# Retention output in an encoder step: the products with v first, then one product per pair of heads with a state on the diagonal of a 128x128 block

## The chip, the cores and the metric

The kernel runs on one core of a Trainium2 chip. A time is device microseconds of one execution. The kernel before was run three times: median 1369.04 us, lowest 1367.47, highest 1370.69. One further execution was recorded by the hardware profiler; its records span 1362.0 us, and all rows shown here come from it. In the rows PE is TensorE, PEld its weight loads, DVE is VectorE, ACT is ScalarE, POOL is GpSimd, SP is SyncE.

## The reference, cut to what matters

Two layers run over 512 prompt frames and 32 sample frames. Each layer has three branches: attention, retention and a gated recurrence. The change touches retention alone, for 8 heads of 64 columns:

```python
inner = jnp.einsum('bnihd,bnjhd->bnhij', q, k) * decay
y_in = jnp.einsum('bnhij,bnjhe->bnihe', inner, v)
...
y_x = jnp.einsum('bnihd,nbhde,hi->bnihe', q, s_prev, xi)
return (y_in + y_x).reshape(b, t, h, d).astype(dt), s_final.astype(s0.dtype)
```

`y_in` is what a block of frames gives its own frames, through v. `y_x` is what all blocks before it give, through the state (64x64 for each head). The sum of both goes on to a normalization per head.

## The kernel before, in words

All activations lie with features on partitions and the 544 frames (512 and 32) along the free dimension. The kernel's main work is a long row of products with 128x128 blocks of weights (`block`, L244). Each float32 weight is split into a high and a low part, the cast on ScalarE (L200) and the difference on VectorE (L201), eight blocks of weights ahead of their use (`LEAD = 8`). A block is three products (high by high, high by low, low by high) for each of two halves of 272 columns, so six matmuls.

Everything else is side work: generators that are resumed between blocks. Each yields the number of blocks to pass before its next step, taken from the table `PACE`. So the order on each engine is written by the program, once, and an engine works its own list in order. A step's place is counted in blocks of weights; nothing in it depends on how long anything takes.

`ret_job` is the side work of retention. It runs once for each layer.

- It makes copies of v and k with frames on partitions (`vt`, `kt`; `vts`, `kts` for the 32 sample frames), through transposes (L322).
- It makes the products of k and v for each block of 128 frames and each head (L574), and copies them to `kv`, half of the tile named `states`.
- It takes the mean over a head's columns off v (POOL, L589 and L591), adds up and decays `kv` (L598, L599), and writes the centred states into `stc`, the other half of `states` (VectorE, L611 and L612). In `stc` head 2p lies on partitions 0 to 63 and head 2p+1 on 64 to 127, each 64 columns wide.
- For each of the four pairs p of heads: eight products of q and k (L635), their mask on VectorE (L638), seven blocks of weights later the output. The output's PSUM tile `pv` is one bank of 128 partitions by 512 columns: head 2p in the upper 64 partitions, 2p+1 in the lower. Block c of 128 columns gets a product with v for each head (L649: 128 rows of weights by 64 columns, 128 columns moved) and, where c > 0, a product with the state for each head (L652: 64 rows by 64 columns, 128 moved). The two kinds alternate. Then ScalarE copies the bank out (L654).
- For the sample frames the same in eight pairs of a product with v (L661: 32 rows by 64 columns, 32 moved) and one with the state (L663: 64 by 64, 32 moved), and a copy (L664).

The operands here are plain float32. The trace holds two PE records for each such product, for instance 128 records of L649 for its 64 products. Below a pass is one such record.

Rotary positions for q are put on beside it (`rope_tile`): a swap by DMA, products on VectorE (L545) and POOL (L546), a sum on VectorE (L548), a scale on POOL (L551, L552). Large tiles come from the pool `slab`, which has 15 places that are given out again when their last reader is done.

Of the kernel before, what the change touches and what calls it, by code (L numbers as in the profile page):

```python
# [13 lines left out]
MUL, ADD, SUB = ALU.mult, ALU.add, ALU.subtract  # L14
# [3 lines left out]
NP, NS = 512, 32  # L18
# [7 lines left out]

# [1 line left out]
BRANCH = {"A": 0, "B": 1, "C": 2}  # L28
# [4 lines left out]
def layer_units():  # L33
    """Units of 128 output features, in groups whose 128x128 blocks are taken in turn. wg stands for the
    recurrence's gates, two to a block, which are used beside the units that follow."""
    u = [[("pl", f)] for f in range(8)]
    u += [[("xr", 0), ("xr", 1)], [("wg", 0)], [("xr", 2)], [("xr", 3)]]
    u += [[("va", t)] for t in range(4)]
    for t in range(4):
        u += [[("qa", t)], [("ka", t)]]  # L40
    u += [[(k, t)] for k in ("kb", "vb", "qb") for t in range(4)]
    for br in "CAB":
        u += [[("z" + br.lower(), t)] for t in range(4)]
        for f in range(8):
            u += [[("g" + br, f)], [("b" + br, f)]]
    u += [[(k, f)] for k in ("wo", "pg") for f in range(8)]
    return u


def blocks_of(kind):  # L50
# [8 lines left out]
LEAD = 8  # L59
# a layer's last units, from this one on, take one half of the columns after the other  # L60
HELD = (6, 2)
WARM = (16, 30, 5)
# blocks to pass between the steps of the side work
PACE = {
# [5 lines left out]
# copies out of PSUM: 1 where the vector engine makes them, 2 where the two engines take turns  # L70
VEC = {"va": 0, "tok": 0, "p0": 0, "p1": 0, "pt": 0, "kv": 0, "pv": 1, "yb": 0}

# [1 line left out]
C_ID, C_O64, C_O1K, C_MK = 0, 128, 256, 384  # L74
# [5 lines left out]

# [1 line left out]
P_CW, P_CB, P_BA, P_BX, P_LAM, P_GN, P_LG, P_LB = 0, 16, 20, 24, 28, 32, 36, 44  # L82
# [29 lines left out]
def bc(ap, dims):  # L112
    """A view of a tile's part: its partitions, then `dims` as [step, count] from its first element."""
    return bass.AP(ap.tensor, ap.offset, [ap.ap[0], *dims])
# [3 lines left out]
def encoder(ctx: ExitStack, tc, xT, pT, W, RB, KC, VC, PAR, CST, o_y, o_k, o_v, o_rp, o_rs, o_cv, o_lr):  # L118
# [17 lines left out]
    def sl(name, dt=F32, shape=(128, 4, N)):  # L136
        return slab.tile(list(shape), dt, tag="slab", name=name)
# [12 lines left out]
    sp = cp.tile([128, 2, L, 4], F32, name="sp")  # L150
# [5 lines left out]

    # ---- side work: generators that are resumed between the blocks of the main products. Each yields the
    # number of blocks to pass before its next step. ----
    jobs = []
    clock = [0]  # L160
# [19 lines left out]

# [1 line left out]
    raw, parts, held = {}, {}, {}  # L182
# [41 lines left out]

    # the next layer's first chunks are split before the normalization takes the engines
    def split_ahead(l):
# [30 lines left out]

    # products that nobody reads keep the tensor engine's clock up where it waits
    def busy(n):
# [3 lines left out]

# [1 line left out]
    st = {"xh": [sl("xh", F32R) for _ in range(2)], "xl": [sl("xl", F32R) for _ in range(2)]}  # L265
# [26 lines left out]

    # 4 softplus(-lambda) and -8 softplus(-lambda)
    def decay_rates():
# [16 lines left out]

# [1 line left out]
    def layer(l, env, nxt):  # L313
# [10 lines left out]

        # token-major copy of a feature-major operand
        def tok_steps(src, tok, toks, d):
# [3 lines left out]

        # -- attention --
        def bias_loads(p):
# [40 lines left out]
        def attn_step(p, qs):  # L373
# [3 lines left out]
            now = [], []  # L377
            # the two heads' products lie in different rows of the array
            for j in range(2):
# [95 lines left out]

        # -- recurrence --
        W547 = NP + 3 + NS
# [32 lines left out]
        def lru_job():  # L510
            R, I, A = env["lru"]
            # s = tanh(4 sp r), a = exp(-8 sp r); 1 - a = s (1 + a), 1 - a^2 = (1 - a)(1 + a)
            for t in range(4):
                S.activation(A[:, t], R[:, t], AF.Exp, scale=sp[:, 1, l, t:t + 1])
                S.activation(R[:, t], R[:, t], AF.Tanh, scale=sp[:, 0, l, t:t + 1])
                yield PACE["lru0"]
            y = I
            for t in range(4):
                r, a = R[:, t], A[:, t]
                V.scalar_tensor_tensor(r, a, 1.0, r, ADD, MUL)  # L520
                V.tensor_scalar(a, r, -1.0, 1.0, MUL, ADD)
                V.scalar_tensor_tensor(r, a, 1.0, r, ADD, MUL)
                yield PACE["lru1"]
            for t in range(4):
                S.activation(R[:, t], R[:, t], AF.Sqrt)
                yield PACE["lru2"]
            for t in range(4):
                G.tensor_tensor(R[:, t], R[:, t], I[:, t], MUL)
                yield PACE["lru3"]
                V.tensor_tensor_scan(y[:, t, :NP], A[:, t, :NP], R[:, t, :NP], 0.0, MUL, ADD)  # L530
                V.tensor_tensor_scan(y[:, t, NP:], A[:, t, NP:], R[:, t, NP:], pcol(P_SL, t), MUL, ADD)
            yield 2
            env["yc"] = y
            Q.dma_start(out=o_lr[l, :, :, 0:1], in_=y[:, :, NP - 1:NP])
            Q.dma_start(out=o_lr[l, :, :, 1:2], in_=y[:, :, N - 1:N])

        # -- retention: q and k carry gamma^(i + 1) and gamma^-(j + 1), i and j counted in their block --
        def rope_tile(key, t, x):
# [17 lines left out]
        def ret_job():  # L556
# [7 lines left out]
            yield from tok_steps(KB, kt, kts, PACE["tok"])  # L564
            # states before the centering of v over a head's columns
            stt_ = sl("states", shape=(128, 2, 16, 64))
            kv, stc = stt_[:, 0], stt_[:, 1]
            kvs = tmp("kvs", (128, 4, 64))
# [41 lines left out]
            yield 3  # L610
            V.tensor_tensor(stc[:, :12], kv[:, :12], bc(smu[:, :12], [[1, 12], [0, 64]]), SUB)  # L611
            V.tensor_tensor(stc[:, 12:], s0, bc(smu[:, 12:], [[1, 4], [0, 64]]), SUB)  # L612
            yield 6
# [3 lines left out]
            mask = cst[:, C_MK:C_MK + 128]  # L617
            # sample
            ins = tmp("ins", (NS, 2, 4, 32))
# [9 lines left out]
            for p in range(4):  # L629
# [12 lines left out]
                yield PACE["y2"]  # L642
                pv = psum("pv")
                for c in range(4):
                    cc = slice(c * 128, c * 128 + 128)
                    for j in range(2):
                        r = slice(64 * j, 64 * j + 64)
                        h = 2 * p + j
                        T.matmul(pv[r, cc], lhsT=vt[:, c, h * 64:h * 64 + 64], rhs=inn[j][:, cc],  # L649
                                 start=True, stop=c == 0)  # L650
                        if c:
                            T.matmul(pv[r, cc], lhsT=stc[r, (c - 1) * 4 + p], rhs=QB[r, p, cc],  # L652
                                     start=False, stop=True)
                copy("yb")(QB[:, p, :NP], pv)  # L654
                yield PACE["y3"]
            pv = psum("pv")
            for h in range(8):
                q, j = h // 2, h % 2
                r = slice(64 * j, 64 * j + 64)
                o = pv[r, q * 32:q * 32 + 32]  # L660
                T.matmul(o, lhsT=vts[:, h * 64:h * 64 + 64], rhs=ins[:, j, q], start=True, stop=False,  # L661
                         tile_position=(0, 64 * j))
                T.matmul(o, lhsT=stc[r, 12 + q], rhs=QB[r, q, NP:], start=False, stop=True)  # L663
            S.copy(QB[:, :, NP:], pv[:, :128].rearrange("p (a b) -> p a b", a=4))  # L664
# [28 lines left out]

        # -- normalization: c, the mean over a quarter of the features, is taken off first; the sums of what is
        # left and of its squares give the mean and the variance. hf: the half of the columns, None for all. --
        def span(hf):
# [83 lines left out]

        # -- what is done with a unit's products --
        KEY = {"ka": "KT", "va": "VA", "qb": "QB", "kb": "KB", "vb": "VB"}
# [104 lines left out]

        # the embedding through its gate; running sums for the normalization
        def gate(t, ps, hf):
# [35 lines left out]

        # units of which one half of the columns is taken after the other; together: block by block of all of
        # them, or one unit after another
        def by_halves(units, together):
# [161 lines left out]
```

## Time and profile before

| | before |
|---|---|
| median of 3 runs | 1369.04 us (1367.47 to 1370.69) |
| profiled execution, span | 1362.0 us |
| its time beside the span | not recorded; the median is 7.0 us above the span |
| PE busy | 1337.0 us, 98%, 10847 instructions |
| PEld busy | 1284.8 us, 94% |
| DVE, ACT, POOL busy | 57%, 44%, 15% |
| mean granted TensorE clock | 0.994 |
| retention's products of the output | L649 x128, L652 x96, L661 x32, L663 x32 records |

A row of the timeline gives a start, a duration from the first start to the last end, the engine, the line, the operation, the tile it writes and reads, the rows*columns of weights, the moved partitions x columns, and how many were merged. Matmuls overlap: one that takes 0.27 us from start to end may have the next one start 0.06 us after it, so durations do not add up. What a stretch costs is read from starts: from the start of the row ahead of it to the start of a row behind it. The rows around 295 to 345 us are the four pairs and the sample frames of the first layer; around 963 to 1015 us are those of the second. The granted clock is a share of full speed in each slice.

### The profile page before, as it was taken

The numbers are of one execution on the slowest core, as the hardware profiler recorded it, in microseconds if no ns is written. First come the engines' busy times: TensorE is split into PE (matmuls) and PEld (weight loads), VectorE is DVE, ScalarE is ACT, GpSimd is POOL, SyncE is SP. The second block draws the span as 40 slices with busy tenths as digits, with TensorE's granted clock in tenths as the row PEclk, the third lists the DMA queues.
The fourth block names the chain that finished last, engine by engine and source line by source line (L and its number), as shares of the span: only waits on it lengthen the run. The fifth ranks groups of instructions, "written<-read, shape, count | busy, mean of one in ns | idle before, by whom it ended". The sixth has DMA issues, their size and how long they took to land.

```text
span 1362.0 us, 26929 instructions
## 1 busy us (share of the span) xinstructions
PE 1337.0 (98%) x10847; PEld 1284.8 (94%) x10847; DVE 780.5 (57%) x1659; ACT 596.8 (44%) x1491; POOL 197.7 (15%) x190
## 2 busy tenths in 40 slices
PE   9999999999999999999999999999999999999985
PEld 9999899997999999999899998999889999999985
DVE  5576563661664453467875756558328544445576
ACT  7765544421642243344476654444126333333343
POOL 0210122200101101002311102132001010110034
PEclk9999999999999999999999999999999999999998
DMA  7233513221122222223112453232112222222201
GB/s 287 63 126 94 175 61 98 87 71 47 63 94 94 93 79 84 103 94 125 63 63 100 86 167 98 76 98 82 50 48 93 94 79 93 78 94 93 93 17 66
DMA packets 44284, 124.95 MB, mean 92 GB/s; under 512 B 9344, under 2 KB 13696, under 8 KB 43520
## 3 DMA queue, kind: packets, MB, share of 16 engines
q1 hardware_dynamic: 44160, 123.24, 27.1%
q8 instruction: 85, 1.39, 0.4%
q14 instruction: 39, 0.32, 0.1%
HBM read 111.52 MB, written 7.24 MB: 87 GB/s over the span
## 4 chain that ended last, share of the span: by engine, by line
PE 88%; DVE 6%; ACT 3%; issue 2%; POOL 0%; DVEq 0%; ACTq 0%; POOLq 0%
PE mm L244 76%; PE pv L413 1%; PE pv L649 1%; PE sc L386 1%; PE pv L652 1%; PE tp L402 1%; ACT wh L200 1%; DVE wl L201 1%; PE sc L635 1%; PE tp L322 1%; DVE held L201 1%; PE mm L262 1%; DVE r L714 1%; DVE r L767 1%; DVE lru_i L530 1%
## 5 line engine op out<-in xcount | busy, mean ns | idle before, releaser
L201 DVE TENSOR_TENSOR wl<-raw,wh 128x256 fp32r<-128x256 f32 x704 | 308.7, 473 | 319.5 <-ACT wh L200 318.7
L244 PE MATMUL mm<-xh,wh 128*128 128x272 f32 x2144 | 456.2, 294 | 0.5 <-ACT xrp L829 0.5
L244 PE MATMUL mm<-xl,wh 128*128 128x272 f32 x2144 | 444.3, 288 | 0.0
L244 PE MATMUL mm<-xh,wl 128*128 128x272 f32 x2144 | 442.4, 287 | 0.4 <-DVE wl L201 0.4
L244 PEld LDWEIGHTS mm<-xh,wh 128*128 128x128 f32 x2144 | 335.1, 188 | 14.6 <-issue 10.6
L244 PEld LDWEIGHTS mm<-xh,wl 128*128 128x128 f32 x2144 | 336.6, 188 | 0.6 <-DVE wl L201 0.6
L244 PEld LDWEIGHTS mm<-xl,wh 128*128 128x128 f32 x2144 | 335.7, 188 | 0.0
L200 ACT CAST wh<-raw 128x256 fp32r<-128x256 f32 x704 | 251.1, 403 | 55.8 <-PE mm L244 52.8
L852 ACT ACTIVATE sg<-mm 128x544 f32<-128x544 f32 x48 | 30.1, 626 | 145.0 <-PE mm L244 145.0
L864 POOL TENSOR_TENSOR m<-m,sg 128x544 f32<-128x544 f32 x30 | 42.5, 1417 | 313.4 <-DVE sg L862 313.4
L244 PE MATMUL mm<-xh,held 128*128 128x272 f32 x320 | 64.8, 296 | 7.1 <-ACT sg L895 5.1
L347 ACT ACTIVATE sx<-sx,sst 128x128 f32<-128x128 f32 (+4 forms) x68 | 37.9, 558 | 68.5 <-DVE sst L345 65.7
L244 PEld LDWEIGHTS mm<-xh,held 128*128 128x128 f32 x320 | 51.7, 192 | 9.3 <-ACT sg L895 5.5
L244 PE MATMUL mm<-ml,wh 128*128 128x272 f32 x256 | 53.0, 288 | 0.0
L244 PE MATMUL mm<-mh,wh 128*128 128x272 f32 x256 | 52.9, 288 | 0.0
L244 PE MATMUL mm<-mh,wl 128*128 128x272 f32 x256 | 52.8, 287 | 0.0
L862 DVE TENSOR_TENSOR sg<-mm,sg 128x544 f32<-128x544 f32 x32 | 23.2, 725 | 41.5 <-PE mm L244 41.5
L244 PE MATMUL mm<-xl,held 128*128 128x272 f32 x160 | 46.7, 292 | 0.0
L255 ACT CAST xh<-r 128x544 fp32r<-128x544 f32 (+1 forms) x32 | 17.0, 532 | 67.6 <-DVE r L879 63.8
L244 PEld LDWEIGHTS mm<-mh,wl 128*128 128x128 f32 x256 | 40.2, 188 | 0.0
L244 PEld LDWEIGHTS mm<-ml,wh 128*128 128x128 f32 x256 | 40.1, 188 | 0.0
L688 POOL TENSOR_TENSOR QB<-QB,sq 128x544 f32<-128x544 f32 x8 | 10.9, 1366 | 200.9 <-DVE sq L686 190.5
(256 smaller groups left out, 1923.4 us busy)
## 6 DMA issues: line engine op xcount, KB each, us to landing
raw<-in_W SPq DMA_DIRECT2D x189, 512.0 KB, 3.2
bias<-in_RB SPq DMA_DIRECT2D x16, 256.0 KB, 4.2
x<-in_xT SPq DMA_DIRECT2D x4, 544.0 KB, 8.6
o_v<-VA SPq DMA_DIRECT2D x2, 1088.0 KB, 4.5
o_k<-KT SPq DMA_DIRECT2D x2, 1088.0 KB, 5.2
swap<-KB SPq DMA_DIRECT2D x32, 68.0 KB, 2.7
swap<-QB SPq DMA_DIRECT2D x32, 68.0 KB, 2.0
o_y<-r SPq DMA_DIRECT2D x6, 272.0 KB, 2.2
```

Of the source, the lines that this page charges most:

```text
L200: S.copy(h, t)
L201: V.tensor_tensor(lo, t, h.bitcast(F32), SUB)
L244: T.matmul(ps[:, hf, :H2], lhsT=w[:, n % 2, :], rhs=x[:, hf * H2:(hf + 1) * H2], start=first and i == 0, stop=last and i == 2)
L255: S.copy(h, src)
L262: T.matmul(ps[:, 0, :H2], lhsT=zero[:, :128], rhs=zero, start=True, stop=True)
L322: T.transpose(tp[:rows, t * 128:(t + 1) * 128], src[:, t, c0:c0 + rows], ident)
L347: S.activation(x, x, AF.Exp, bias=s[:, 0:1], scale=-1.0, accum_out=s[:, 1:2])
L386: T.matmul(scs[j][:, o:o + n], lhsT=q_[r, p, i * 128:i * 128 + 128], rhs=k_[r, p, :n], start=k == 0, stop=k == 2)
L402: T.transpose(tp[:, c:c + 128], xs[j][:, c:c + 128], ident)
L852: S.activation(halves(sg), pv, AF.Sigmoid)
L862: V.tensor_tensor(halves(sg), pv, halves(sg), MUL)
L864: (V if kind == "bB" and t == 7 else G).tensor_tensor(m, m, sg, ADD)
```

## The change

The states lie in a tile of their own, `std`, 16 blocks of 128x128. A block is for one pair of heads: head 2p's state in its upper left 64x64 quarter, head 2p+1's in its lower right one, and zeros in the two others. The zeros come from a memset on POOL ahead of the products of k and v. VectorE writes the quarters in four instructions of 64 partitions in place of two of 128. `kv` becomes a tile of its own.

The output of a pair begins with all eight products with v. The three products with a state follow: one for both heads, 128 rows by 128 columns. The first product in each half of the bank clears it, all others add to it, and the last ends the group: one accumulation group for the bank. The sample frames go the same way: eight products with v, then four with a state. Comments were taken out, too, and lines moved by four.

```diff
-            stt_ = sl("states", shape=(128, 2, 16, 64))
-            kv, stc = stt_[:, 0], stt_[:, 1]
+            kv = sl("kv", shape=(128, 16, 64))
+            std = sl("states", shape=(128, 16, 128))
+            G.memset(std, 0.0)
...
-            V.tensor_tensor(stc[:, :12], kv[:, :12], bc(smu[:, :12], [[1, 12], [0, 64]]), SUB)
-            V.tensor_tensor(stc[:, 12:], s0, bc(smu[:, 12:], [[1, 4], [0, 64]]), SUB)
+            for j in range(2):
+                r = slice(64 * j, 64 * j + 64)
+                V.tensor_tensor(std[r, :12, 64 * j:64 * j + 64], kv[r, :12], bc(smu[r, :12], [[1, 12], [0, 64]]), SUB)
+                V.tensor_tensor(std[r, 12:, 64 * j:64 * j + 64], s0[r], bc(smu[r, 12:], [[1, 4], [0, 64]]), SUB)
...
                 for c in range(4):
                     cc = slice(c * 128, c * 128 + 128)
                     for j in range(2):
-                        r = slice(64 * j, 64 * j + 64)
                         h = 2 * p + j
-                        T.matmul(pv[r, cc], lhsT=vt[:, c, h * 64:h * 64 + 64], rhs=inn[j][:, cc],
-                                 start=True, stop=c == 0)
-                        if c:
-                            T.matmul(pv[r, cc], lhsT=stc[r, (c - 1) * 4 + p], rhs=QB[r, p, cc],
-                                     start=False, stop=True)
+                        T.matmul(pv[64 * j:64 * j + 64, cc], lhsT=vt[:, c, h * 64:h * 64 + 64], rhs=inn[j][:, cc],
+                                 start=c == 0, stop=False)
+                for c in range(1, 4):
+                    cc = slice(c * 128, c * 128 + 128)
+                    T.matmul(pv[:, cc], lhsT=std[:, (c - 1) * 4 + p], rhs=QB[:, p, cc], start=False, stop=c == 3)
...
-            for h in range(8):
-                q, j = h // 2, h % 2
-                r = slice(64 * j, 64 * j + 64)
-                o = pv[r, q * 32:q * 32 + 32]
-                T.matmul(o, lhsT=vts[:, h * 64:h * 64 + 64], rhs=ins[:, j, q], start=True, stop=False,
-                         tile_position=(0, 64 * j))
-                T.matmul(o, lhsT=stc[r, 12 + q], rhs=QB[r, q, NP:], start=False, stop=True)
+            for q in range(4):
+                for j in range(2):
+                    h = 2 * q + j
+                    T.matmul(pv[64 * j:64 * j + 64, q * 32:q * 32 + 32], lhsT=vts[:, h * 64:h * 64 + 64],
+                             rhs=ins[:, j, q], start=q == 0, stop=False, tile_position=(0, 64 * j))
+            for q in range(4):
+                T.matmul(pv[:, q * 32:q * 32 + 32], lhsT=std[:, 12 + q], rhs=QB[:, q, NP:], start=False, stop=q == 3)
```

In the order of instructions two places matter. The first is PE's list at the first pair of heads in the first layer. `mm` takes the main products, `pv` is the output's bank, `inner` the masked products of q and k, `vbtok` v with frames on partitions, `QB` q; sizes are those of the output. Before:

```order
L244 MATMUL mm<-zch,wl 128x272 x2
L649 MATMUL pv<-inner,vbtok 64x128 x3
L652 MATMUL pv<-QB,states 64x128
L649 MATMUL pv<-inner,vbtok 64x128
L652 MATMUL pv<-QB,states 64x128
L649 MATMUL pv<-inner,vbtok 64x128
L652 MATMUL pv<-QB,states 64x128
L649 MATMUL pv<-inner,vbtok 64x128
L652 MATMUL pv<-QB,states 64x128
L649 MATMUL pv<-inner,vbtok 64x128
L652 MATMUL pv<-QB,states 64x128
L649 MATMUL pv<-inner,vbtok 64x128
```

One more L652 follows, and then L244 again; the other pairs are alike. Now, at the fourth pair of the same layer, with the sample frames behind it:

```order
L244 MATMUL mm<-zch,wl 128x272 x2
L653 MATMUL pv<-inner,vbtok 64x128 x8
L657 MATMUL pv<-QB,states 128x128 x3
L244 MATMUL mm<-zch,wh 128x272 x2
L244 MATMUL mm<-zcl,wh 128x272 x2
L244 MATMUL mm<-zch,wl 128x272 x2
L664 MATMUL pv<-ins,vbtoks 64x32 x8
L667 MATMUL pv<-QB,states 128x32 x4
L244 MATMUL mm<-zch,wh 128x272 x2
```

Fourteen products in twelve rows have become eleven in two, and the blocks of weights around them stand where they stood. The second place is POOL's list, at the rotary positions of q in the first layer; + marks what is new:

```order
 L551 TENSOR_TENSOR QB<-QB,cst 128x512 [waits DVE_49,Activation_49]
 L552 TENSOR_TENSOR QB<-QB,cst 128x32
+L569 MEMSET states 128x2048 [waits PE_49]
 L546 TENSOR_TENSOR swap<-swap,cst 128x544 [waits DMAHW6_49,DMAHW7_49,DMAHW5_49,DMAHW0_49]
 L551 TENSOR_TENSOR QB<-QB,cst 128x512 [waits DVE_49,Activation_49]
```

The memset has gone in between the second and the third tile of q, and waits for PE alone, for the last reader of the tile that had the place before it.

## The prediction

> **What bounds the kernel now.** I read the page's chain of waits first, then the table of busy time around the change, then PE's timeline.
>
> ```profile
> span 1362.0 us, 26929 instructions
> PE 88%; DVE 6%; ACT 3%; issue 2%; POOL 0%; DVEq 0%; ACTq 0%; POOLq 0%
> ```
>
> PE is 88% of the chain that ended last. The table of stretches has one for the retention's output of layer one (columns: length, then busy time with counts of PE, PEld, DVE, ACT, POOL, then granted clock, DMA share, GB/s):
>
> ```profile
> 295.00:345.00 50.00, 50.00 (x368) 39.56 (x367) 12.02 (x26) 10.74 (x27) 0.00 (x0) 0.97 0.09 32
> ```
>
> PE is never idle in these 50 us, DVE and ACT are busy for 12 and 11, POOL not at all, and DMA has 9%. A microsecond that PE saves here moves all that follows; nothing else is near its limit. PEld's 39.56 says that PE is not at its best: 10 us pass in which no weights load. PE's timeline at the first pair of heads shows where:
>
> ```profile
> 295.11 0.41 PE L244 MATMUL mm<-zch,wl 128*128 128x272 f32 x2
> 295.45 0.65 PE L649 MATMUL pv<-inner,vbtok 128*64 128x128 f32 x6
> 296.03 0.43 PE L652 MATMUL pv<-QB,states 64*64 64x128 f32 x2
> 296.39 0.43 PE L649 MATMUL pv<-inner,vbtok 128*64 128x128 f32 x2
> ...
> 299.64 0.43 PE L652 MATMUL pv<-QB,states 64*64 64x128 f32 x2
> 300.00 0.52 PE L244 MATMUL mm<-zch,wh 128*128 128x272 f32 x2
> 300.36 0.41 PE L244 MATMUL mm<-zcl,wh 128*128 128x272 f32 x2
> 300.61 0.41 PE L244 MATMUL mm<-zch,wl 128*128 128x272 f32 x2
> ```
>
> Two passes of L244 take 0.25 us (300.36 to 300.61). From 295.11 to 300.36 are 5.25 us; less two such rows of L244, the group costs 4.75 us. A product of two passes takes 0.36 us wherever the kind changes (296.03 to 296.39). The same products with v without a change stand in the attention:
>
> ```profile
> 126.47 0.42 PE L244 MATMUL mm<-xh,wl 128*128 128x272 f32 x2
> 126.81 1.09 PE L413 MATMUL pv<-sx,vatok 128*64 128x128 f32 x16
> 128.19 0.41 PE L244 MATMUL mm<-xl,wh 128*128 128x272 f32 x2
> ...
> 135.30 0.41 PE L244 MATMUL mm<-xh,wl 128*128 128x272 f32 x2
> 135.64 0.88 PE L413 MATMUL pv<-sx,vatok 128*64 128x128 f32 x12
> 136.80 0.41 PE L244 MATMUL mm<-xl,wh 128*128 128x272 f32 x2
> ```
>
> Counted in the same way (1.72 and 1.50, each less 0.50), 16 passes cost 1.22 us and 12 cost 1.00: 0.055 a pass, and 0.34 for going from 128x128 weights to 128x64 and back. So the old group is 28 passes at 0.055, which is 1.54, and 3.21 us for 13 changes of shape (in, eleven within, out), 0.25 each.
>
> **The change part by part: pairs of heads.** The new group has two changes of shape, since L657's 128x128 weights have the shape of L244's. Its 16 passes with v are the 1.22 us above, both changes in. The six passes with 128x128 float32 weights and 128 columns moved are new in this place. Nearest rows: transposes of that size, and the weight loads of real float32 products of that size in the normalization (the second fence is PEld).
>
> ```profile
> 236.70 0.41 PE L244 MATMUL mm<-xh,wl 128*128 128x272 f32 x2
> 236.95 0.60 PE L322 MATMUL tp<-cst,KB 128*32 128x128 f32 x4
> 237.64 0.41 PE L244 MATMUL mm<-xl,wh 128*128 128x272 f32 x2
> ```
>
> ```profile
> 680.44 0.76 PEld L748 LDWEIGHTS tp<-cst,lnst 128*128 128x128 f32 x6
> ```
>
> Four transposes cost 0.94 less 0.50, 0.11 each. L748's six loads end 0.76 us after the first begins; less the 0.19 of the last, five steps of 0.114. I take 0.11: the product is L748's kind. Low bound: 0.055, as with 64 columns. High: 0.125, L244's own step. So the new group is 1.22 + 6 x 0.11 = 1.88 us (1.55 to 1.97, and 2.13 with two changes of 0.25 in place of 0.34) against 4.75. It saves 2.87 us (2.62 to 3.20); eight groups save **23.0 us** (21.0 to 25.6). They are alike by L649's records, which keep to 272 ns in both layers:
>
> ```profile
> L649 PE MATMUL pv<-inner,vbtok x128: 272/273/323, 295.5 to 1003.9; 128*64 128x128 f32 x128
> ```
>
> [...]
>
> **Sample frames.** The old stretch, and what follows it:
>
> ```profile
> 336.77 0.41 PE L244 MATMUL mm<-zch,wl 128*128 128x272 f32 x2
> 337.12 0.30 PE L661 MATMUL pv<-ins,vbtoks 32*64 32x32 f32 x2
> 337.34 0.30 PE L663 MATMUL pv<-QB,states 64*64 64x32 f32 x2
> ...
> 341.11 0.66 PE L244 MATMUL mm<-zcl,wh 128*128 128x272 f32 x2
> 341.57 0.65 PE L244 MATMUL mm<-zch,wl 128*128 128x272 f32 x2
> ...
> 344.64 0.41 PE L244 MATMUL mm<-xh,wh 128*128 128x272 f32 x2
> ```
>
> From 336.77 to 341.11, less 0.50, the stretch costs 3.84 us. A pass of 32 columns is read from the attention's sample frames:
>
> ```profile
> 171.58 0.42 PE L469 MATMUL sc<-PT,kvc 128*64 128x32 f32 x8
> 171.94 0.30 PE L469 MATMUL sc<-PT,vatoks 32*64 32x32 f32 x4
> 172.17 0.43 PE L469 MATMUL sc<-PT,kvc 128*64 128x32 f32 x8
> ```
>
> Eight take 0.36, four take 0.23, each with a change: 0.0325 a pass. New: 16 x 0.0325 = 0.52, changes in and out 0.34, eight passes on 128x128 weights at 0.11, 0.88; 1.74 us. Saved 2.10 a layer (high cost: passes of 0.055 and 0.125, changes of 0.25, 2.38, saves 1.46; low: 0.055 for the eight, saves 2.54). Twice: **4.2 us** (2.9 to 5.1).
>
> **The clock behind it.** From 341.11 to 344.64 stand eight rows of two passes: 3.53 us where 2.00 are normal. The granted clock says why, in both layers (length, PE busy, clock, DMA, GB/s):
>
> ```profile
> 342.00:344.00 2.00, 2.00 (x10) 0.50 0.00 0
> ...
> 1010.00:1012.00 2.00, 2.00 (x11) 0.53 0.00 0
> ```
>
> The clock falls to half behind the 3.64 us of 32-column passes and comes back. Behind the attention's 2.35 us of such passes it stays (five engines, then clock):
>
> ```profile
> 172.00:174.00 2.00, 2.00 (x42) 1.71 (x41) 1.18 (x3) 0.79 (x3) 2.00 (x4) 1.00 0.00 0
> ```
>
> The new stretch is 1.7 us with half of it full-width weights, and the 4.5 us of thin work before it becomes 1.9. I take it that the clock stays: 1.53 x 2 = **3.1 us** (0 to 3.1). [...]
>
> **Added work.** POOL gets one memset of 2048 elements a layer:
>
> ```profile
> L364 POOL MEMSET bias<- 64x64 f32 x16 | 2.2, 145 | 80.2 <-DMA bias<-in_RB 68.1 <-PE mm L244 12.0
> ...
> L552 POOL TENSOR_TENSOR QB<-QB,cst 128x32 f32<-128x32 f32 x8 | 3.5, 435 | 0.0
> ```
>
> At L364's 145 ns for 64 elements it takes at most 4.6 us, less if part of the 145 is fixed. Queued behind it is L546 for the third tile of q, for which DVE's L548 waits, with DVE's L201 behind:
>
> ```profile
> 237.84 1.35 POOL L546 TENSOR_TENSOR swap<-swap,cst 128x544 f32<-128x544 f32 x1
> ...
> 243.03 0.72 DVE L548 TENSOR_TENSOR QB<-QB,swap 128x544 f32<-128x544 f32 x1
> ```
>
> L546 ends at 239.19, L548 begins at 243.03: 3.8 us of cover, and behind it PE holds split weights for eight blocks (6 x 0.125 x 8 = 6.0 us). Cost: nothing. On DVE two instructions become four of as many columns, so twice the time:
>
> ```profile
> L611 DVE TENSOR_TENSOR states<-states,mu x2: 950/951/952, 283.5 to 951.9; 128x768 f32<-128x768 f32 x2
> ```
>
> With its smaller neighbour for the last block that is about 1.4 us more at 285 us, ten before PE reads the states at 296, and within the 6.0 us of split weights: nothing. In the changed program's list of tiles, the tiles that follow find readers of their places that are long done, so the second slab place costs nothing either.
>
> **Sum.** 23.0 + 4.2 + 3.1 = 30.3 us off the profiled 1362.0: 1331.7. The median lies 7.0 above the span: **1338.7 us**.
>
> **Rivals.** *The clock still dips* (or dips elsewhere, as its slices shift): without the 3.1 us, 1341.8. For it: the four groups of thin work remain, if shorter; against: the 172 to 174 row. *Weight loads in series*: a full-width float32 pass in this place takes a load and a matmul one after the other, 0.19 + 0.27 = 0.46. A group is then 1.22 + 2.76 = 3.98, saves 0.77, eight save 6.2; the sample frames lose 0.7 a layer. With the dip gone, 1361. Against it: L748's 0.114. *PE's gain is not passed on*, since another engine becomes the bound: about 1369; against it the 12 and 11 us of 50. *Slower, by the memset*: at L552's 13.6 ns an element it takes 28 us; the third tile of q is 24 us late, DVE stands at L548, PE runs out of split weights after 6 and loses 18 us in each layer: 1338.7 + 36 = 1375. It costs from 10 us on and eats the gain from 25 on. Against it: L364 has 2.3 ns an element. That the change does something else is out: the list of PE shows eight and three products in place of the alternation.
>
> **How the numbers follow.** Forecast 76%, dip stays 14%, series 4%, not passed on 3%, slower 3%. The range: the unknown costs give savings from 21.0 + 2.9 + 0 to 25.6 + 5.1 + 3.1, which are 23.9 and 33.8 us, so 1335.2 to 1345.1; I widen by 1 us for the scatter of the median (1367.5 to 1370.7 in three runs): 1334 to 1346. That holds the first two cases, some 0.85. A measurement here can't tell less than about 0.2% (2.7 us) from no change; the first three cases are beyond it: faster 0.94, same 0.03, slower 0.03.
>
> **What would show it.** In PE's timeline of the changed kernel: L653 as one row of 16 passes of about 0.9 us, L657 as six passes 0.11 apart, the next L244 at most 2 us after the first L653; steps of 0.46 would mean series loads. Behind the sample frames L244 at 0.25 a row, clock 1.00. POOL's memset below 5 us, and L548 not late. PE busy down by some 30 us. Wrong it would be if the span fell by less than 24 us, or if PE waited for L201 near 245 us.

## The result and the profile after

| | before | after |
|---|---|---|
| median | 1368.26 us (1366.26 to 1370.69, 4 runs) | 1335.96 us (1333.96 to 1339.12, 4 runs) |
| profiled execution: span | 1362.0 us | 1332.2 us |
| its mean granted clock | 0.994 | 0.993 |
| PE busy, PEld busy | 1337.0, 1284.8 us | 1307.9, 1272.4 us |

The ratio is 0.9759, 95% interval 0.9739 to 0.9778: 32.3 us off the median. In a second series it was 0.9772 (0.9755 to 0.9788). The forecast was 1338.7 us, the range 1334 to 1346.

The page after, head, busy line and shares of the chain of waits:

```profile
span 1332.2 us, 26812 instructions
PE 1307.9 (98%) x10783; PEld 1272.4 (96%) x10783; DVE 778.8 (58%) x1663; ACT 596.6 (45%) x1491; POOL 201.9 (15%) x192
PE 89%; DVE 6%; ACT 3%; issue 2%; POOL 0%; DVEq 0%; ACTq 0%; POOLq 0%
```

PE's busy time fell by 29.1 us, the span by 29.8. PE still is 89% of the chain, so what PE saved went through to the end. PE's timeline after, at the first pair of heads, with the one row of PEld that belongs to it:

```profile
295.11 0.41 PE L244 MATMUL mm<-zch,wl 128*128 128x272 f32 x2
295.45 1.09 PE L653 MATMUL pv<-inner,vbtok 128*64 128x128 f32 x16
296.47 0.94 PE L657 MATMUL pv<-QB,states 128*128 128x128 f32 x6
297.16 0.50 PE L244 MATMUL mm<-zch,wh 128*128 128x272 f32 x2
297.50 0.41 PE L244 MATMUL mm<-zcl,wh 128*128 128x272 f32 x2
```

```profile
296.47 0.74 PEld L657 LDWEIGHTS pv<-QB,states 128*128 128x128 f32 x6 [0.17 <-issue]
```

From the start of the L244 row ahead (295.11) to the second one behind (297.50) are 2.39 us; less the 0.50 of two such rows, the group costs 1.89, where it was 4.75. Six loads end 0.74 us after the first begins; less the last's 0.19 (the L244 load right behind it takes that), five steps of 0.11. The sample frames after:

```profile
325.31 0.41 PE L244 MATMUL mm<-zch,wl 128*128 128x272 f32 x2
325.79 0.65 PE L664 MATMUL pv<-ins,vbtoks 32*64 32x32 f32 x16
326.37 1.08 PE L667 MATMUL pv<-QB,states 128*128 128x32 f32 x8
327.29 0.49 PE L244 MATMUL mm<-zch,wh 128*128 128x272 f32 x2
327.62 0.41 PE L244 MATMUL mm<-zcl,wh 128*128 128x272 f32 x2
327.87 0.41 PE L244 MATMUL mm<-zch,wl 128*128 128x272 f32 x2
```

The same count gives 2.31 less 0.50, 1.81 us where it was 3.84. The next L244 rows come 0.25 apart: the clock did not fall behind it (granted clock 1.00 in each window from 325 to 333 us, and from 976 to 984 us in the second layer).

How far PE is ahead at a later place is read from the first product of the group norm: of before (L681) and of after (L685), all 32 of them, with the first and the last start.

```profile
L681 PE MATMUL sc<-sqh,o x32: 283/288/291, 350.7 to 1038.9; 128*128 128x272 f32 x32
```

```profile
L685 PE MATMUL sc<-sqh,o x32: 282/288/293, 335.6 to 1009.4; 128*128 128x272 f32 x32
```

15.1 us are won by the first one of the first layer, 29.5 by the last one of the second, 29.8 by the end. Each layer gives its half, and nothing of it is lost behind them.

The memset on POOL, and what is queued behind it; the last row is VectorE's:

```profile
237.84 1.82 POOL L569 MEMSET states<- 128x2048 f32 x1
239.61 1.36 POOL L546 TENSOR_TENSOR swap<-swap,cst 128x544 f32<-128x544 f32 x1
243.06 0.72 DVE L548 TENSOR_TENSOR QB<-QB,swap 128x544 f32<-128x544 f32 x1
```

L546 starts 1.77 us later than before, and L548 at 243.06 where it stood at 243.03.

### The profile page after: what moved, and what is told of

Same layout as the page of the kernel before. It is cut to its first block, busy times and chain, and to the rows that moved or that the text cites. A ratio compares the mean times of both kernels' runs of the same rounds, so it can differ in the third digit from the quotient of the medians.

```text
span 1332.2 us, 26812 instructions
## 1 busy us (share of the span) xinstructions
PE 1307.9 (98%) x10783; PEld 1272.4 (96%) x10783; DVE 778.8 (58%) x1663; ACT 596.6 (45%) x1491; POOL 201.9 (15%) x192
## 4 chain that ended last, share of the span: by engine, by line
PE 89%; DVE 6%; ACT 3%; issue 2%; POOL 0%; DVEq 0%; ACTq 0%; POOLq 0%
PE mm L244 78%; PE pv L413 2%; PE sc L386 1%; PE tp L402 1%; PE sc L639 1%; PE tp L322 1%; DVE held L201 1%; PE pv L653 1%; ACT wh L200 1%; PE mm L262 1%; DVE wl L201 1%; DVE r L718 1%; PE pv L657 1%; PE pv L497 0%; DVE s L923 0%
## 5 line engine op out<-in xcount | busy, mean ns | idle before, releaser
L244 PE MATMUL mm<-xh,wh 128*128 128x272 f32 x2144 | 455.4, 294 | 0.5 <-ACT xrp L833 0.5
L244 PE MATMUL mm<-xl,wh 128*128 128x272 f32 x2144 | 443.5, 288 | 0.0
L244 PE MATMUL mm<-xh,wl 128*128 128x272 f32 x2144 | 442.1, 287 | 0.4 <-DVE wl L201 0.4
L244 PEld LDWEIGHTS mm<-xh,wh 128*128 128x128 f32 x2144 | 334.3, 188 | 13.9 <-issue 9.9
L244 PEld LDWEIGHTS mm<-xh,wl 128*128 128x128 f32 x2144 | 335.9, 188 | 0.6 <-DVE wl L201 0.6
L244 PEld LDWEIGHTS mm<-xl,wh 128*128 128x128 f32 x2144 | 335.0, 188 | 0.0
L244 PE MATMUL mm<-xh,held 128*128 128x272 f32 x320 | 64.8, 296 | 6.8 <-ACT sg L899 5.1
L244 PEld LDWEIGHTS mm<-xh,held 128*128 128x128 f32 x320 | 51.6, 192 | 9.0 <-ACT sg L899 5.5
L244 PE MATMUL mm<-ml,wh 128*128 128x272 f32 x256 | 52.9, 288 | 0.0
L244 PE MATMUL mm<-mh,wl 128*128 128x272 f32 x256 | 52.8, 288 | 0.0
L244 PE MATMUL mm<-mh,wh 128*128 128x272 f32 x256 | 52.7, 287 | 0.0
L244 PE MATMUL mm<-xl,held 128*128 128x272 f32 x160 | 46.6, 291 | 0.0
L244 PEld LDWEIGHTS mm<-mh,wl 128*128 128x128 f32 x256 | 40.1, 188 | 0.0
L244 PEld LDWEIGHTS mm<-mh,wh 128*128 128x128 f32 x256 | 40.1, 188 | 0.0
L244 PEld LDWEIGHTS mm<-ml,wh 128*128 128x128 f32 x256 | 40.0, 188 | 0.0
```

The costliest lines, as they stand in the source:

```text
L244: T.matmul(ps[:, hf, :H2], lhsT=w[:, n % 2, :], rhs=x[:, hf * H2:(hf + 1) * H2], start=first and i == 0, stop=last and i == 2)
```

## The experiments

The theories: the gain comes from the order, since each change between two shapes of weights costs PE some 0.25 us (A), or it comes from something that only the diagonal gives. The clock falls because of the thin work of the sample frames alone, or only with the alternating pairs ahead of it. The memset is free because it is covered, not because a memset on POOL never matters. Each diff is against the changed kernel. Where runs of different chips are compared, I take the ratio to the kernel before on the same chip.

**The order without the diagonal.** The states are multiplied head by head again, from 64x64 quarters of the blocks, but behind the products with v.

```diff
-                    T.matmul(pv[:, cc], lhsT=std[:, (c - 1) * 4 + p], rhs=QB[:, p, cc], start=False, stop=c == 3)
+                    for j in range(2):
+                        r = slice(64 * j, 64 * j + 64)
+                        T.matmul(pv[r, cc], lhsT=std[r, (c - 1) * 4 + p, 64 * j:64 * j + 64], rhs=QB[r, p, cc],
+                                 start=False, stop=c == 3)
```

> The order of the change without its diagonal: eight products with v first, then six products with a 64x64 state (two to a block of columns, taken from the quarters of the same tile) in place of three full ones; the sample frames as in the change. Changes of shape cost 0.25 us each (theory A): the group has three (in, from 128x64 to 64x64, out) and 28 passes at 0.055 us, some 2.2 to 2.3 us from one L244 to the next against 1.89 in the change and 4.75 before; over eight groups 3 us more than the change, about 1339 us by the median. If products on different quarters of the array run side by side as soon as no other shape stands between them (theory B), the twelve state passes take half the time, the group about 1.95 us, no difference from the change. If the 0.25 us hangs on each new product with 64 rows, whatever stands before it (theory C), the group has six of them at 0.36, some 3.2 us, and the run is 10 us above the change.

Measured: 1336.25 us (1335.07 to 1337.78), ratio 0.9752 (0.9737 to 0.9767), the same as the change's. PE's timeline at the first pair:

```profile
295.68 0.41 PE L244 MATMUL mm<-zch,wl 128*128 128x272 f32 x2
296.02 1.09 PE L653 MATMUL pv<-inner,vbtok 128*64 128x128 f32 x16
297.05 0.87 PE L659 MATMUL pv<-QB,states 64*64 64x128 f32 x12
297.85 0.51 PE L244 MATMUL mm<-zch,wh 128*128 128x272 f32 x2
298.20 0.41 PE L244 MATMUL mm<-zcl,wh 128*128 128x272 f32 x2
```

The group takes 2.52 less 0.50, 2.02 us. So of the 2.86 us that the change saves in a group, the order gives 2.73 and the diagonal 0.13; over eight groups the diagonal is worth 1.0 us, too little to be seen in the medians. That the gain needs the diagonal falls. The twelve passes with 64x64 weights took 0.80 us (297.05 to 297.85) with the change of shape behind them in it.

The group was forecast at 2.2 to 2.3 us by theory A and at 1.95 by theory B. The rows above merge many records; the single ones show why 2.02 lies between. The passes of L653 begin at 296.022, 296.029, 296.182, 296.189, 296.291 and 296.298 us and so on: two at a time, 0.007 apart, and from the second couple on the next two 0.109 later. Those of L659 do the same (297.046, 297.053, 297.206, 297.213, 297.315, 297.322). The two passes of one product that stands alone begin at least 0.109 us apart, so the two of such a couple belong to two products, and these are the two heads of the pair, which write the two halves of the bank. They run side by side. So 0.055 a pass, and the 0.06 us from one start to the next that I named for the timeline, are half of 0.109 for two. In the kernel before only the first four passes of a group come in couples (295.452, 295.458, 295.612, 295.618). After that each product stands between two of the other kind, and its passes run alone (295.721 and 295.830). So theory B is right in that products run side by side. Its 1.95 came from halving 0.055, which is already the price of a pass in a couple.

**The diagonal without the order.** Two products with v and a full state product in turn, block by block.

```diff
-                for c in range(1, 4):
-                    cc = slice(c * 128, c * 128 + 128)
-                    T.matmul(pv[:, cc], lhsT=std[:, (c - 1) * 4 + p], rhs=QB[:, p, cc], start=False, stop=c == 3)
+                    if c:
+                        T.matmul(pv[:, cc], lhsT=std[:, (c - 1) * 4 + p], rhs=QB[:, p, cc], start=False, stop=c == 3)
```

> The diagonal of the change without its order: in each block of columns two products with v, then the full 128x128 state product, so the shapes alternate; the sample frames as in the change. Theory A (a price for each change of shape, in both directions): a group has six changes in place of two, four more at 0.25 us, 2.9 us in place of 1.89; eight groups, 8 us above the change, about 1344 us. Theory D (the wait comes from adding to columns of PSUM that were written just before): only the step from a v product to the state product of the same columns waits, the step back to other columns does not; 4 us above the change at most. If the diagonal alone made the gain, the run equals the change.

Measured: 1341.59 us (1340.15 to 1343.4), ratio 0.9791 (0.9776 to 0.9806), by the ratios 4.4 us above the change. PE's timeline at the first pair:

```profile
295.27 0.41 PE L244 MATMUL mm<-zch,wl 128*128 128x272 f32 x2
295.61 0.66 PE L653 MATMUL pv<-inner,vbtok 128*64 128x128 f32 x8
296.20 0.49 PE L656 MATMUL pv<-QB,states 128*128 128x128 f32 x2
296.61 0.44 PE L653 MATMUL pv<-inner,vbtok 128*64 128x128 f32 x4
296.98 0.49 PE L656 MATMUL pv<-QB,states 128*128 128x128 f32 x2
...
298.35 0.41 PE L244 MATMUL mm<-zcl,wh 128*128 128x272 f32 x2
```

The group takes 3.08 less 0.50, 2.58 us: four more changes of shape than in the change's group cost 0.69, 0.17 each. Both directions cost: eight passes with v take 0.59 with the change behind them (296.20 less 295.61), 0.15 above 8 x 0.055; two state passes take 0.41 (to 296.61), 0.19 above 2 x 0.11. A cost that arises only when a product adds to what another kind has just written would show in one direction, so that falls. A change of shape has a price here, but 0.17 us and not 0.25.

The rest of the 0.25 is the running side by side that the old order prevents; here the products with v still come in couples (296.614, 296.621, 296.774, 296.781). If a couple or a pass alone is counted at 0.109 us and a full-width pass at 0.11, the old group has 2 couples and 24 passes alone, 2.83 us, and 1.92 are left for its 13 changes, 0.15 each. In the same way a change comes to 0.16 us in the order without the diagonal, and to 0.17 here and in the change itself. So of the 2.73 us that the order gives, some 1.3 come from twelve products that now share their time with another, and some 1.4 from ten changes fewer. This is an estimate from the starts; no run separates the two. The start flags were changed together with the order, too. A change of shape is not dearer with the old flags (0.15 us) than with the new (0.16 and 0.17), so they don't look like a part of the gain; no run changes them alone.

**The parts by themselves.** In the first kernel the pairs are as in the change and the sample frames alternate as before; in the second it is the other way round.

```diff
...
-            for q in range(4):
-                T.matmul(pv[:, q * 32:q * 32 + 32], lhsT=std[:, 12 + q], rhs=QB[:, q, NP:], start=False, stop=q == 3)
+            for h in range(8):
...
+                T.matmul(o, lhsT=vts[:, h * 64:h * 64 + 64], rhs=ins[:, j, q], start=True, stop=False,
+                         tile_position=(0, 64 * j))
+                T.matmul(o, lhsT=std[r, 12 + q, 64 * j:64 * j + 64], rhs=QB[r, q, NP:], start=False, stop=True)
```

> The change for the four pairs of heads; the sample frames alternate between 32x64 and 64x64 weights as before. The sample stretch costs 3.84 us again in place of 1.81 in each layer: 4 us more than the change. The clock: if the 3.6 us of 32-column passes alone make it fall (theory E), it is at half for some 3.4 us behind 326 and 980 us, 3 us more, together 7 us above the change, about 1343. If it takes the thin work of the pairs ahead of it too (theory F), the clock stays at 1.00 there: 4 us, about 1340.

Measured: 1343.66 us (1341.05 to 1347.78), ratio 0.9799 (0.978 to 0.9818). The clock fell, although the pairs ahead no longer alternate. Windows of PE in the first layer (length, PE busy, clock, DMA, GB/s), then its rows there:

```profile
328.00:330.00 2.00, 2.00 (x16) 0.71 0.00 0
330.00:332.00 2.00, 2.00 (x10) 0.50 0.00 0
332.00:334.00 2.00, 2.00 (x11) 0.50 0.00 0
334.00:336.00 2.00, 2.00 (x12) 0.58 0.16 45
```

```profile
326.06 0.27 PE L665 MATMUL pv<-ins,vbtoks 32*64 32x32 f32 x2
326.26 0.30 PE L667 MATMUL pv<-QB,states 64*64 64x32 f32 x2
...
330.12 0.82 PE L244 MATMUL mm<-zch,wh 128*128 128x272 f32 x2
330.74 0.66 PE L244 MATMUL mm<-zcl,wh 128*128 128x272 f32 x2
```

From the first of these four windows to the last, 0.58 + 1.00 + 1.00 + 0.84 = 3.42 us of full clock are missing. In the second layer 1.70 us are missing (990 to 996 us). The stretch of the sample frames is enough to make the clock fall.

```diff
+                        r = slice(64 * j, 64 * j + 64)
...
-                        T.matmul(pv[64 * j:64 * j + 64, cc], lhsT=vt[:, c, h * 64:h * 64 + 64], rhs=inn[j][:, cc],
-                                 start=c == 0, stop=False)
...
+                        T.matmul(pv[r, cc], lhsT=vt[:, c, h * 64:h * 64 + 64], rhs=inn[j][:, cc],
+                                 start=True, stop=c == 0)
+                        if c:
+                            T.matmul(pv[r, cc], lhsT=std[r, (c - 1) * 4 + p, 64 * j:64 * j + 64], rhs=QB[r, p, cc],
+                                     start=False, stop=True)
```

> The pairs of heads alternate as before; the sample frames as in the change. Each of the eight groups costs 4.75 us again: 23 us above the change. Theory E: the clock does not fall behind the sample frames, since their stretch is 1.8 us: about 1359 us, 9 us under the kernel before. Theory F (thin work of pairs and sample frames together makes it fall): it still falls in one layer or both, 1 to 3 us more.

Measured: 1357.44 us (1356.38 to 1358.4), ratio 0.9906 (0.9891 to 0.9921). In this second kernel the alternating pairs are back at the old price, and behind the new stretch of the sample frames the clock stays (1.00 from 336 to 346 us and from 1000 to 1012 us):

```profile
337.23 0.65 PE L665 MATMUL pv<-ins,vbtoks 32*64 32x32 f32 x16
337.82 1.08 PE L668 MATMUL pv<-QB,states 128*128 128x32 f32 x8
338.73 0.50 PE L244 MATMUL mm<-zch,wh 128*128 128x272 f32 x2
339.07 0.42 PE L244 MATMUL mm<-zcl,wh 128*128 128x272 f32 x2
339.32 0.41 PE L244 MATMUL mm<-zch,wl 128*128 128x272 f32 x2
```

So the clock stayed at 1.00 here through the groups of 4.7 us that alternate at 128 columns (294 to 336 us), and in the kernel before it fell to 0.50 behind the 3.84 us that alternate at 32 columns (342 to 344 us). By the ratios the kernel is 20.1 us above the change; the two profiled executions, which have nearly the same clock (0.994 and 0.993), are 22.4 apart. The eight groups make 22.9. Taken from the before of the same chip (1369.94), the pairs alone save 26.3 us and the sample frames alone 12.5, together some 6 more than the change does. The products in them are 22.9 and 4.1. The rest goes with the clock, whose mean was 0.985 to 0.989 in the runs of before, 0.985 to 0.991 with the pairs alone and 0.991 to 0.994 with the sample frames alone; why the two gains of clock do not add up is not shown.

**The stretch of the sample frames made twice.** Pairs as in the change; the sixteen alternating products of the sample frames are made a second time over the first result.

```diff
...
-            for q in range(4):
-                T.matmul(pv[:, q * 32:q * 32 + 32], lhsT=std[:, 12 + q], rhs=QB[:, q, NP:], start=False, stop=q == 3)
+            for h in [*range(8), *range(8)]:
...
```

> The pairs as in the change; the sample frames alternate as before, and their sixteen products are made twice, the second time over the first's result, so the stretch of 32-column passes is 7.4 us in place of 3.7. Theory E' (the clock falls when a window of fixed length, that runs on its own, holds thin work only): 3.7 us of it fell in one of two layers, 1.8 us in none; 7.4 us holds a whole window wherever it lies, so the clock falls in both layers, and begins to fall inside the stretch. If instead the clock answers to single events or to chance, one of the two layers may well stay at 1.00. Time: 2 x 5.6 us of added work against the change, and 3 to 7 us of slow clock, about 1351.

Measured: 1359.05 us (1358.94 and 1359.16), ratio 0.9908 (0.9879 to 0.9937). PE's windows in the first layer:

```profile
330.00:340.00 10.00, 10.00 (x52) 0.50 0.00 0
340.00:350.00 10.00, 10.00 (x81) 0.99 0.14 54
```

5.12 us of full clock are missing in this place, and 5.12 in the second layer. The clock fell in both layers and while the stretch (326.06 to 335.04 in the first) was still running, as theory E' has it. All amounts of this kind are near multiples of 1.7: 1.70, 3.42, 5.12. At half clock 1.7 us are lost in 3.4, so the clock seems to be set for about 3.4 us at a time. In the profile of before it is at half from 341.09 to 344.50 us and from 1010.10 to 1013.52, 3.41 each time. Its falls at 341.09, 1010.10 and 1310.48 lie 196.0 and 88.0 times 3.413 us apart, which fits windows of fixed length that run on their own. That such a window holds thin work only is not shown: with the pairs alone the clock fell at 328.84 by the windows above, and up to 326.06, within the last 3.41 us, PE still had rows of L244. By the records PE was busy ahead of the fall in the doubled stretch, 3.94 of 4.00 us from 326 to 330. A fall in one of two layers, which the expectation names for 3.7 us, is not what the profiles show: before the change (0.50 and 0.53) and with the pairs alone (0.50 and 0.50) it fell in both.

The time was some 8 us above what I expected. The two places cost 9.8 us each against the change's profile, 5.6 of it products, which is 19.6 where I had reckoned 14 to 18. The rest is lost late in the two layers, where the change's profile is at half clock too, but for half as long: 3.4 us of clock are missing at 670 to 680 and as much at 1302 to 1310, where the change lacks 1.7 in each.

**The memset, five and sixteen times.** The same zeros are written again.

```diff
-            G.memset(std, 0.0)
+            for _ in range(5):
+                G.memset(std, 0.0)
```

> The change with its memset of the states made five times (1.81 us each in the change's profile, so 9.1 us in each layer on POOL). The prediction held that the memset is covered up to about 10 us: VectorE's sum for the third tile of q (L548) waits for POOL's L546, which stands behind the memset, and the split weights for eight blocks last 6 us. With five, L546 ends near 248.2 us and L548 begins 5 us late; if the cover is as reckoned, PE waits for nothing near 245 us and the time is that of the change (about 1336). If VectorE's delay reaches PE at once, 5 us a layer, about 1346.

Measured: 1336.77 us (1336.41 and 1337.14), ratio 0.9746 (0.9717 to 0.9774). POOL's and VectorE's timeline:

```profile
238.08 9.29 POOL L570 MEMSET states<- 128x2048 f32 x5
247.33 1.35 POOL L546 TENSOR_TENSOR swap<-swap,cst 128x544 f32<-128x544 f32 x1
248.72 0.72 DVE L548 TENSOR_TENSOR QB<-QB,swap 128x544 f32<-128x544 f32 x1 [5.35 <-POOL swap L546]
```

VectorE now stands 5.35 us for the swap, and PE does not notice: it is busy for 2.00 us in each window of two from 236 to 262 us. With 16 in place of 5:

> The change with its memset made sixteen times, 29 us in each layer on POOL: the prediction's slower rival at its price. L548 begins some 25 us late; PE works on for 6 us from the weights that are split, then stands for 18 to 19 us in each layer: about 1336 + 37 = 1373 us, slower than the kernel before. If PE had more weights in hand than eight blocks, or VectorE were not held by L548, it would be nearer to 1336.

Measured: 1376.69 us (1374.24 to 1382.37, 8 runs), ratio 1.0051 (1.003 to 1.0072), half a per cent slower than before the change. POOL, VectorE and PE there:

```profile
268.45 1.32 POOL L546 TENSOR_TENSOR swap<-swap,cst 128x544 f32<-128x544 f32 x1
269.81 0.73 DVE L548 TENSOR_TENSOR QB<-QB,swap 128x544 f32<-128x544 f32 x1 [25.82 <-POOL swap L546]
270.92 0.82 PE L244 MATMUL mm<-xh,wl 128*128 128x272 f32 x2 [16.73 <-DVE wl L201]
```

The wait goes from POOL through VectorE to PE's split weights, as the rival in the prediction had it: 16.7 us in each layer. The L244 behind it runs at half clock for a while (0.82 where 0.41 is normal, granted clock 0.50 up to 278 us), and the kernel is 39.9 us above the one with five memsets beside it, where the two waits make 33.4. So the memset is free for its size, and the cover ends between 9.3 and 29.8 us of it.

**Fewer changes of shape still.** States first (they have the shape of L244), then v, then the next pair's products of q and k right behind; the attention's sample frames with all 128-row products first.

```diff
...
-    "y2": 1, "y3": 1, "gn": 8, "gn1": 2, "gn2": 6, "gn3": 2}
+    "y2": 1, "y3": 0, "gn": 8, "gn1": 2, "gn2": 6, "gn3": 2}
...
+                for c in range(1, 4):
+                    cc = slice(c * 128, c * 128 + 128)
+                    T.matmul(pv[:, cc], lhsT=std[:, (c - 1) * 4 + p], rhs=QB[:, p, cc], start=c == 1, stop=False)
...
-            for p in range(4):
-                for kt in range(3):
...
+            for kts in ((0, 1), (2,)):
+                for p in range(4):
+                    for kt in kts:
...
```

> The change, with still fewer changes of shape: in a pair's group the three full-width state products come first, then the eight with v, and the next pair's products of q and k stand right behind them (one block of weights less between, PACE y3 from 1 to 0); and the attention's sample frames make all their products of 128 rows first and those of 32 rows behind them. Saved, if a change of shape costs 0.1 to 0.25 us: one return to 128x128 for each pair, some 0.25 x 6; and six changes of 0.11 in each layer for the attention's sample frames, 1.3; together 2.5 to 3 us under the change, a ratio of about 0.974 to before. If the weight loads of the first state products are not ready ahead, or the next pair's products wait for the mask's tiles, nothing is gained.

Measured: 1338.66 us (1337.5 to 1340.48), ratio 0.9785 (0.9771 to 0.9798). The change, run again beside it:

> The change itself, on the same chip as the next kernel, for comparison: a ratio of 0.976 to the kernel before, and an execution's time spread by some 5 us with the number of stretches at half clock.

Measured: 1335.93 us (1334.21 to 1339.43), ratio 0.9772. PE's timeline of the kernel with fewer changes, a pair of heads and the attention's sample frames:

```profile
171.84 1.13 PE L470 MATMUL sc<-PT,kvc 128*64 128x32 f32 x32
172.90 0.65 PE L470 MATMUL sc<-PT,vatoks 32*64 32x32 f32 x16
173.48 0.52 PE L244 MATMUL mm<-xh,wh 128*128 128x272 f32 x2
...
294.90 0.83 PE L652 MATMUL pv<-QB,states 128*128 128x128 f32 x6
295.66 1.09 PE L657 MATMUL pv<-inner,vbtok 128*64 128x128 f32 x16
296.68 1.16 PE L640 MATMUL sc<-QB,KB 64*128 64x128 f32 x16
297.77 0.52 PE L244 MATMUL mm<-zch,wh 128*128 128x272 f32 x2
...
322.32 0.65 PE L665 MATMUL pv<-ins,vbtoks 32*64 32x32 f32 x16 [0.82 <-ACT QB L659]
```

The steps did what they should: a pair with its q and k takes 2.98 us, where the change has 3.18 in two places; the attention's stretch 1.84 in place of 2.55. But only three pairs of a layer have products of q and k behind them. Behind the fourth the sample frames now follow at once, and PE waits 0.82 us for ScalarE's copy of that pair's bank (L659). The fourth pair with the sample frames takes 4.25 us (319.40 to 324.15, less 0.50), where the change takes 1.89 and 1.81. So in each layer the pairs win 3 x 0.20 us and lose 0.55, and what is left is the attention's 2 x 0.71 = 1.4 us.

Counted at the same block of weights, PE is 0.8 us ahead of the change run beside it at 646 us, before the layer norm (0.3 of it from the very start), and 2.35 behind at 672. Between them, at 660 to 668 us, 3.4 us of clock are missing that the other has. It is still 2.2 behind at 1018 us, and 2.6 at the end (spans 1336.7 and 1334.1). Why the clock falls in one of two programs that are alike in that place is not settled. The run does not say that fewer changes of shape are worse; it says that a gain of 1.4 us was smaller than what the clock took.

## Why the prediction was right

- **The group of a pair**: 1.88 us forecast, 1.89 measured. The pass at 0.11 is confirmed by PEld's row. The pass at 0.055 (half of a couple) and the 0.34 for in and out, taken from the attention, hold in the retention.
- **The sample frames**: 1.74 forecast, 1.81 measured; 2.03 us saved in a layer in place of 2.10.
- **The clock behind them**: it stays at 1.00, in both layers, and that is the sample stretch's own doing. Together with the products that is 8 x 2.86 + 2 x 2.03 + 2 x 1.53 = 30.0 us, and the group norm's rows show 29.5 of it by 1009 us.
- **The rival by which the clock dips elsewhere** came true in part. In the profile after, half clock shows at 662 to 668 us (0.69, 0.50 and 0.96), in a layer norm where it was full before (1.00), and the missing 1.7 us cost about 0.4 on PE's way to the second layer: 28.1 us were won by the end of that layer's sample frames where the terms give 28.5.
- **The memset**: 1.81 us, far below the bound of 4.6. The terms of the slower rival hold too: 28 us were reckoned to cost 18 us a layer, 29.8 us cost 16.7 and some clock.
- **Weight loads in series** fall with the 0.11.

The forecast does not reckon with small products that run side by side. The trace shows them: as soon as products of one kind follow one another, those of 64 columns start in couples, 0.007 us apart, and a couple takes 0.109 us where a full-width pass takes 0.11. Six couples of state passes need about 0.66 us, as the six full-width passes do. So the diagonal neither loses nor gains by it. The 0.13 us that it saves in a group is about the price of the one change of shape that it spares.

One step failed: "the median lies 7.0 above the span". In the runs whose span is on record the time is about 1.8 us above it (1333.96 to 1332.2). The other 5.2 us came from setting one execution's span against another execution's time: the profiled one had more clock than the others. The runs of before on record have spans of 1363.4 to 1371.6 with a mean clock of 0.984 to 0.992; the profiled one had 1362.0 and 0.994. The sum was right for the profiled pair, 29.8 us measured for 30.3, but the median fell by 32.3. An estimate of the rest from the clocks: in the last series the median clock was 0.9865 of 1367 us before and 0.991 of 1334 after, that is 18.5 and 12.0 us of full clock missing. The difference of 6.5 us is twice the 3.1 that the prediction had in the two places it could see. With 26.9 us for the products that makes 33.4, near the 32.65 measured there; some of the missing clock lies at the end (0.50 from 1356 us on in the profile of before), where PE waits anyway. In which stretches the other executions of before lost it is not on record; whether it was behind the sample frames too stays open. So the forecast was 2.7 us too high: 2.0 from this gain (32.3 against 30.3), and the rest since the median of before had come down from 1369.04 to 1368.26 with a fourth run.

And the mechanism was only half right. The prediction took 3.21 us of the old group for 13 changes of shape, 0.25 each. By the starts a change costs 0.15 to 0.17, and the rest is the time of twelve products that had to run alone. The sum did not rest on it: the old group was read as a whole, and the new one was built from whole stretches of the attention, in which the products already run in couples.

## What to carry to other kernels

Group PE's small products by the shape of their weights, with those for the two halves of a bank next to each other, before joining them into full blocks: here the order gave 2.73 us of each 2.86, about half of it, by the estimate above, by products that run side by side, and the joining 0.13. A merged row hides that; look at the starts of single records. Read what a stretch costs from the starts of the rows around it, and take the price of a new stretch from a whole stretch of that form elsewhere in the trace. Before a span is set against a median, compare the mean clock of the profiled execution with that of the runs; and if a step runs on an idle engine, look at what stands behind it in the queue and how far that may slip.

## What was not expected

The clock fell while PE was busy by the records: windows with 2.00 us of PE in 2.00 went to 0.50. What brought it down was 3.84 us of float32 products of 32 columns between small weights; groups of 4.7 us with 128 columns and 13 changes of shape did not. The loss comes in portions of about 1.7 us (half clock for 3.4), one or two behind the same stretch in the two layers of one execution, three behind the doubled one. The spread between runs of one kernel goes with it: the change's runs at a mean clock of 0.993 took 1333.96 to 1334.21 us, those at 0.988 took 1338.83 to 1339.43.
